# Gates in f32, shift sums as matmul rows, a softplus moved to the head, conditioning sums moved, and the chunk inverse applied inside the chain

## The chip, the cores and the metric

The kernel runs on one core of a Trainium2 chip. The metric is the device time of one execution in microseconds. Five engines work in parallel, each through its own queue: TensorE (PE, matmuls), VectorE (DVE, elementwise and scans), ScalarE (ACT, activations and copies), GpSimd (POOL) and SyncE (SP), which here issues nearly all DMAs.

## What is computed

Two residual layers of width 1024 over 1024 positions, and behind them a third, hybrid layer that the change does not touch. In front of the first two stands an RMS norm with a scale and a shift that come from a conditioning vector:

```
c_act = silu(c)
for i in range(2):
    cond = c_act @ ada_w[i] + ada_b[i]          # 1024 x 3072
    shift, scale, gate = cond[:D], cond[D:2*D], cond[2*D:]
    h = rmsnorm(x, norm_g[i]) * (1.0 + scale) + shift
    out = rglru_block(h) if i == 0 else gated_deltanet_block(h)
    x = x + gate * out
```

The first layer is a gated recurrence. Its gates are block-diagonal, eight blocks of 128x128:

```
xb, zg = split(h @ in_w);  xf = causal_conv4(xb) + conv_b
gates  = sigmoid(einsum('sni,knij->ksnj', xf, gate_w) + gate_b)      # r, i
log_a  = -8 * r * softplus(-lam);  a = exp(log_a)
b      = sqrt(-expm1(2 * log_a)) * (i * xf)
y      = scan(a, b) * silu(zg);   out = y @ out_w
```

The second is a gated delta rule with eight heads of 128, in chunks. Per chunk T is the inverse of a unit lower triangular matrix, and the state S passes from chunk to chunk:

```
w = T @ (k_beta * exp(g));  u = T @ v_beta
v_new = u - w @ S
o     = q_dec @ S + attn @ v_new
S     = S * e_last + k_dec.T @ v_new
```

## The kernel before

Activations lie transposed (channels on partitions). A projection is made of f16 products: the f32 weight is staged in `wst`, and `split` makes a high part `wh` (ACT) and a low part `wl` (DVE) of it; three matmuls of 512 columns (L111 to L113) add up to one f32 product. The framework fixes the order of the instructions on each engine ahead of time from the program's order, its priorities and buffers, and each engine runs its list in order.

*First layer.* A conditioning sum is made on DVE: a stage of `ada_w` (`sta`, 128x8x256, or `ast` and `wst_ada`) is multiplied by a column of `ccol` and accumulated, one instruction for each of eight row blocks (`ada_acc`, L148 and L150); transposes on PE (`ps_ada`) and a DVE reduction finish it into `adac`. `ada_load(0)` makes the shift so, and its f16 pair `shl` multiplies the projection weights once (`ps_sh`) for a bias. `xbranch(p)`, four of them, makes projection, convolution `xf` (L331), gates and scan for 256 channels; `zbranch(p)` makes the other half. Between them stand `ada_step()`s, which finish one pending sum (`ada_fin`, L185 to L189) and start the next. In `xbranch`, `xf` is split into `xh` and `xl`, and each gate is three matmuls (L501 to L503). The softplus of `lam` (`lamn`, some 33 small DVE instructions) is written ahead of the first `xbranch`. Two halves of one sum of the second layer (`ada_part(1, 2, h)`) stand in the loop of the output projection, `out0`.

*Second layer.* `dense(h)` makes q, k and v of a head, `stage1(h)` the products inside chunks, `base(h)` the inverse of the 32-blocks by 31 steps on DVE, `levels(h)` the larger blocks of the inverse `TdT` and behind them u (`ps_u`) and w (`ps_w`) of all eight chunks; `chain(h)` then goes over the chunks with the state S:

```
pe.matmul(ps1[:, :P], wT, S, start=True, stop=True)
pe.matmul(pso[:, :P], qT[:, c, :], S, start=True, stop=False)
dve.scalar_tensor_tensor(out=vn, in0=ps1[:, :P], scalar=nD[:, c:c + 1], in1=u, op0=ALU.mult, op1=ALU.add)
...
pe.matmul(psk[:, :P], kd, vn, start=True, stop=True)
```

The chain of head h is written ahead of `dense(h + 2)` and of the stages of head h + 1, and in the order its instructions lie between theirs.

Of the kernel before, what the change touches and what calls it, by code (L numbers as in the profile page):

```python
# [9 lines left out]
F16 = mybir.dt.float16  # L10
# [10 lines left out]
NK = 8  # L21
# [7 lines left out]
def kernel(ctx, tc, ins, out):  # L29
# [135 lines left out]
    def ada_sum(pl, tiles, l, part, h):  # L165
        acc = pl.tile([P, 512], F32, tag="ad", name="ad")
# [5 lines left out]
    def ada_part(pl, l, part, h):  # L172
        acc = pl.tile([P, 512], F32, tag="ad", name="ad", bufs=2)
# [173 lines left out]
    with ExitStack() as s0:  # L347
# [44 lines left out]

        G0 = pl.tile([P, NK], F32, name="G0")
# [6 lines left out]

        load_x(0)
        prows = load_cols(pl, PA, 0)
# [32 lines left out]
        ada_load(0)  # L435
# [7 lines left out]
    with ExitStack() as sy:  # L443
        ypool = mkpool("y0", stack=sy)
        yT = []
        with ExitStack() as s0:
# [4 lines left out]
            for g2 in range(2):  # L451
                gst = wstage("gst")
                sp.dma_start(gst[:, :D].rearrange("p (n j) -> p n j", n=NK),
                             a["lru_gate_w"][0, g2].rearrange("n i j -> i n j"))
                gh = pl.tile([P, D], F16, name=f"gwh{g2}")
                gl = pl.tile([P, D], F16, name=f"gwl{g2}")
                split(gh, gl, gst[:, :D], scale=WS)
                gw.append((gh, gl))
            lamn = pl.tile([P, NK], F32, name="lamn")
            sp.dma_start(lamn, a["lru_lambda"].rearrange("o (k p) -> p (o k)", p=P))  # L460
            dve.tensor_scalar(out=lamn, in0=lamn, scalar1=-1.0, scalar2=None, op0=ALU.mult)
            softplus(pl, lamn, spl, [P, NK], "sl")
            sp8 = cst.tile([P, NK], F32, name="sp8")
            sp4 = cst.tile([P, NK], F32, name="sp4")
            dve.tensor_scalar(out=sp8, in0=spl, scalar1=-8.0, scalar2=None, op0=ALU.mult)
            dve.tensor_scalar(out=sp4, in0=spl, scalar1=-4.0, scalar2=None, op0=ALU.mult)


            def xbranch(p, w):
                xf = xf0 if p == 0 else lru_xf(p, pl)  # L470
                xh = pl.tile(PR, F16, tag="xh", name="xh")
                xl = pl.tile(PR, F16, tag="xl", name="xl")
                if p > 0:
                    sb = shift_proj(w)
                for e in range(2 if p > 0 else 0):
# [4 lines left out]
                    split(xh[:, e], xl[:, e], xf[:, e])  # L480
                if p == 0:
                    sb = shift_proj(w)
                    for e in range(2):
# [7 lines left out]
                        split(xh[:, e], xl[:, e], xf[:, e])  # L491
                tg = []
                for g2 in range(2):
                    gx = pl.tile(PR, F32, tag=f"gt{g2}", name=f"gt{g2}")
                    gh, gl = gw[g2]
# [45 lines left out]
            adt, adp = [ada_fetch(pl, *adq.pop(0))], []  # L541

            def ada_step():
                if adp:
# [9 lines left out]
            ada_step()  # L554
            xbranch(1, wx[1])
            wx.append(load_w(a["lru_in_w"][0], 3 * WC))
            ada_step()
# [12 lines left out]
            zbranch(3, wz[3])  # L570
        with ExitStack() as s0:
# [7 lines left out]
            for i in range(NT + 1):  # L579
# [27 lines left out]
    with ExitStack() as s0:  # L607
# [28 lines left out]
        eg = gcol.tile([P, NT, NH], F32, name="eg")  # L636
# [7 lines left out]
        act.activation(eg, gc, AF.Exp)  # L644
# [27 lines left out]
        B3 = [P, 4, P]  # L672

        def bc(t, b):
            return t[:, 4 * b:4 * b + 4].unsqueeze(2).to_broadcast(B3)

        def dense(h):
# [3 lines left out]
            for nm in ("q", "k", "v"):  # L681
                xp = pl.tile([P, T + 3], F32, tag="xp", name="xp", bufs=2)
                xt = (pl if nm == "q" else plA).tile([P, T], F32, tag=nm + "T", name=nm + "T", bufs=3 if nm == "q" else 1)
# [14 lines left out]
        def stage1(h):  # L698
# [16 lines left out]
            nD = gcol.tile([P, NT], F32, tag="nD", name="nD", bufs=3)  # L715
# [3 lines left out]
            for n, src in ((0, kT), (1, qT)):  # L719
# [9 lines left out]
                if n == 0:  # L729
# [3 lines left out]
                    dve.tensor_scalar(out=nD, in0=Dc, scalar1=-1.0, scalar2=None, op0=ALU.mult)  # L733
# [41 lines left out]
            st_[h] = dict(qT=qT, attnT=E, U=U, kr=kr, vr=vr, Dc=Dc, nD=nD, rq=rq, Lp=Lp)  # L775
# [22 lines left out]
        def levels(h):  # L798
            d = st_[h]
            U, kr, vr, Dc = d["U"], d["kr"], d["vr"], d["Dc"]  # L800
# [47 lines left out]
            d["wT"], d["u"] = [], []  # L848
            for b in range(2):
                bs = slice(4 * b, 4 * b + 4)  # L850

                def lvl(lh, rh, nm):
                    ps = ps_c(nm)
                    for c in range(4):
                        pe.matmul(ps[:, P * c:P * (c + 1)], lh[:, c, :], rh[:, c, :], start=True, stop=True)
                    return ps.rearrange("p (c t) -> p c t", c=4)
# [3 lines left out]
                for c in range(4):  # L860
# [6 lines left out]
                d["wT"].append(wT)  # L867
                d["u"].append(u)

        def chain(h):  # L870
            d = st_.pop(h)
            qT, attnT, kr, nD, rq = d["qT"], d["attnT"], d["kr"], d["nD"], d["rq"]
# [5 lines left out]
            for c in range(NT):  # L878
                u, wT = d["u"][c // 4][:, c % 4, :], d["wT"][c // 4][:, c % 4, :]
                pso = ps_c("ps_o")  # L880
                if c == 0:
                    vn = u
                else:
                    ps1 = ps_c("ps_ws")
                    pe.matmul(ps1[:, :P], wT, S, start=True, stop=True)
                    pe.matmul(pso[:, :P], qT[:, c, :], S, start=True, stop=False)
                    vn = gcol.tile([P, P], F32, tag="vn", name="vn", bufs=2)
# [62 lines left out]
        def yload(q):  # L950
            if q < NH // 2 - 1:
                for e in range(2):
                    tag = ("kT", "vT", "GB", "Lp", "U", "vr")[2 * q + e]
                    yt = plA.tile([P, 2, T], F16, tag=tag, name="yo", bufs=2 if tag in ("U", "vr") else 1)
# [3 lines left out]
        dense(0)  # L958
        dense(1)
        for h in range(NH):  # L960
            stage1(h)
# [603 lines left out]
```

## Time and profile before

| | before |
|---|---|
| median of 3 runs | 1854.75 us (1852.91 to 1855.04) |
| profiled execution | 1849.51 us |
| its span | 1847.8 us |
| mean granted clock of TensorE | 0.985 of full speed |
| PE, DVE, ACT busy | 1740.0, 1451.2, 937.9 us |

The span runs from the first to the last instruction of the profiled execution; the 1.7 us around it are launch and end. Durations in the rows below are of that execution. Busy time counts an engine's instructions once where they overlap, so a matmul's duration is longer than the distance to the next one; where the text needs the price of a matmul in a full queue, it takes the distance of two starts. An f32 matmul leaves two records.

### The profile page before, as it was taken

Reading aid. Unit: us, or ns where it says so; the run is one execution under the profiler, and the core shown is the slowest. Engines: PE = TensorE matmul, PEld = TensorE weight load, DVE = VectorE, ACT = ScalarE, POOL = GpSimd, SP = SyncE. Lnnn points to the kernel's source line nnn. Section 1 sums busy time; section 2 is a strip of 40 time slices with the busy share of each in tenths; the row PEclk is TensorE's granted clock in tenths of the full one; section 3 lists DMA queues with packets and bytes.
Section 4 is the critical chain, followed back from the end, with each engine's and each line's share of the span. In section 5 each row is a group of like instructions: output and inputs, shape, how many; then the busy total and the mean of one; then the engine's idle time right before and its main releaser. Section 6 shows DMA issues by size and latency. Waiting matters only on the chain.

```text
span 1847.8 us, 29435 instructions
## 1 busy us (share of the span) xinstructions
PE 1740.0 (94%) x11719; PEld 1081.4 (59%) x11719; DVE 1451.2 (79%) x2480; ACT 937.9 (51%) x1669; POOL 66.2 (4%) x152
## 2 busy tenths in 40 slices
PE   4778999989899999999999999999999999999998
PEld 2333449845466655688889586555444444444487
DVE  5898778754898888988566799999999999593332
ACT  6477773345566766676453434655561221572221
POOL 0000010000000000001000110000000000000000
PEclk9889999999999999999999999999999999999999
DMA  9465336413131221335252411101321121111222
GB/s 312 161 156 129 69 103 199 138 55 83 32 92 45 56 77 44 95 110 152 81 183 81 99 49 49 53 19 53 125 80 35 48 90 50 42 33 59 80 70 92
DMA packets 157858, 165.25 MB, mean 89 GB/s; under 512 B 41886, under 2 KB 136158, under 8 KB 157722
## 3 DMA queue, kind: packets, MB, share of 16 engines
q1 hardware_dynamic: 156314, 159.17, 28.7%
q0 software_dynamic: 1408, 4.21, 0.6%
q8 instruction: 92, 1.51, 0.4%
q14 instruction: 44, 0.36, 0.1%
HBM read 139.05 MB, written 23.12 MB: 88 GB/s over the span
## 4 chain that ended last, share of the span: by engine, by line
PE 52%; DVE 30%; ACT 9%; issue 6%; DMA 2%; SPq 0%; POOL 0%; DVEq 0%; ACTq 0%; POOLq 0%
DVE cc L1035 5%; PE psmm L112 4%; PE psmm L111 4%; PE psmm L113 4%; DVE wl L105 3%; PE ps_out L120 2%; PE ps_out L118 2%; PE ps_out L119 2%; DVE tm L790 2%; DVE Tt L792 2%; PE ps_fin L120 2%; PE ps_fin L118 2%; PE ps_fin L119 2%; PE ps_zc L113 1%; PE ps_zc L111 1%
## 5 line engine op out<-in xcount | busy, mean ns | idle before, releaser
L111 PE MATMUL psmm<-hTh,wh 128*128 128x512 f16 x896 | 341.4, 382 | 7.8 <-ACT zs L533 5.3
L112 PE MATMUL psmm<-hTl,wh 128*128 128x512 f16 x896 | 342.0, 382 | 0.6 <-DVE hTl L398 0.6
L113 PE MATMUL psmm<-hTh,wl 128*128 128x512 f16 x896 | 341.7, 381 | 0.0
L1035 DVE SCALAR_TENSOR_TENSOR cc<-cu,cols,cc 128x1024 f32<-128x1024 f32 (+1 forms) x270 | 302.0, 1167 | 0.9
L112 PEld LDWEIGHTS <-wh 128*128 128x128 f16 x1568 | 154.0, 98 | 178.6 <-issue 10.9
L113 PEld LDWEIGHTS <-wl 128*128 128x128 f16 x1568 | 154.0, 98 | 176.0 <-issue 7.5
L111 PEld LDWEIGHTS <-wh 128*128 128x128 f16 x1568 | 154.0, 98 | 173.4 <-issue 6.9
L105 DVE SCALAR_TENSOR_TENSOR wl<-wst,wh 128x2048 f16<-128x2048 f32 (+2 forms) x71 | 153.9, 2171 | 69.8 <-ACT wh L104 69.8
L104 ACT ACTIVATE wh<-wst 128x2048 f16<-128x2048 f32 (+2 forms) x71 | 128.7, 1814 | 102.3 <-PE ps_gs L112 27.7
L790 DVE TENSOR_TENSOR tm<-Lp,Tt 128x248 f32<-128x248 f32 (+30 forms) x248 | 77.3, 312 | 4.1
L792 DVE TENSOR_TENSOR Tt<-Tt,tm 128x248 f32<-128x248 f32 (+30 forms) x248 | 76.7, 309 | 4.7
L119 PE MATMUL ps_z<-wh,hTl 128*128 128x256 f16 x256 | 69.8, 273 | 0.0
L118 PE MATMUL ps_z<-wh,hTh 128*128 128x256 f16 x256 | 69.8, 273 | 0.0
L120 PE MATMUL ps_z<-wl,hTh 128*128 128x256 f16 x256 | 69.8, 273 | 0.0
L118 PE MATMUL ps_fin<-wh,merged 128*128 128x256 f16 x256 | 69.8, 273 | 0.0
L119 PE MATMUL ps_fin<-wh,merged 128*128 128x256 f16 x256 | 69.8, 273 | 0.0
L120 PE MATMUL ps_fin<-wl,merged 128*128 128x256 f16 x256 | 69.8, 273 | 0.0
L119 PE MATMUL ps_out<-wh,hs 128*128 128x256 f16 x256 | 69.7, 273 | 0.0
L118 PE MATMUL ps_out<-wh,hs 128*128 128x256 f16 x256 | 69.7, 273 | 0.0
L120 PE MATMUL ps_out<-wl,hs 128*128 128x256 f16 x256 | 69.7, 273 | 0.0
L123 ACT ACTIVATE hTh<-ps_ht 128x512 f16<-128x512 f32 x32 | 17.4, 594 | 76.0 <-PE ps_ht L271 76.0
L727 ACT ACTIVATE jk<-ps_tk 128x128 f32<-128x128 f32 x128 | 35.7, 279 | 38.6 <-PE ps_tk L723 35.7
(539 smaller groups left out, 4085.9 us busy)
## 6 DMA issues: line engine op xcount, KB each, us to landing
wst<-in_w_in_dram SPq DMA_DIRECT2D x24, 1024.0 KB
wst<-in_gdn_in_w_dram SPq DMA_DIRECT2D x16, 1024.0 KB
ast<-in_ada_w_dram SPq DMA_DIRECT2D x24, 512.0 KB
xt<-in_x_dram SPq DMA_DIRECT2D x16, 512.0 KB
wst<-in_lru_in_w_dram SPq DMA_DIRECT2D x8, 1024.0 KB
sta<-in_ada_w_dram SPq DMA_DIRECT2D x8, 1024.0 KB
wst<-in_lru_out_w_dram SPq DMA_DIRECT2D x4, 1024.0 KB
wst_ada<-in_ada_w_dram SPq DMA_DIRECT2D x4, 1024.0 KB
```

The lines of the kernel that those rows point to most:

```text
L104: act.activation(hi, st, AF.Copy, scale=WS)
L105: dve.scalar_tensor_tensor(out=lo, in0=st, scalar=WS, in1=hi, op0=ALU.mult, op1=ALU.subtract)
L111: pe.matmul(ps, wh[:, k, c0:c0 + P], ah(k), start=(k == 0), stop=False)
L112: pe.matmul(ps, wh[:, k, c0:c0 + P], al(k), start=False, stop=False)
L113: pe.matmul(ps, wl[:, k, c0:c0 + P], ah(k), start=False, stop=(k == nk - 1))
L118: pe.matmul(ps, ah(k), wh[:, k, :], start=(k == 0), stop=False)
L119: pe.matmul(ps, al(k), wh[:, k, :], start=False, stop=False)
L120: pe.matmul(ps, ah(k), wl[:, k, :], start=False, stop=(k == nk - 1))
L727: act.activation(jk, pst[:, P * c:P * (c + 1)], AF.Square, accum_out=kq[:, n, 4 * b + c:4 * b + c + 1])
L790: dve.tensor_tensor(out=tv, in0=Lp[:, j, j + 1:].unsqueeze(1).to_broadcast([P, 8, n]), in1=Tt[:, :, j:j + 1].to_broadcast([P, 8, n]), op=A ...
L792: dve.tensor_tensor(out=Tt[:, :, j + 1:], in0=Tt[:, :, j + 1:], in1=tv, op=ALU.subtract)
L1035: dve.scalar_tensor_tensor(out=acc, in0=cus[j][:, i + t0:i + t0 + n], scalar=col("cw", j, i), in1=acc, op0=ALU.mult, op1=ALU.add)
```

## The change

1. Gates: the gate weights are loaded straight into f32 tiles `gw0` and `gw1` (no stage, no split), `xf` is no longer split, and each gate is one f32 matmul.
2. Shift sums: `ada_load(0)` becomes `ada_rows(0)`. A column of `ccol` is the stationary operand and a 256-column piece of `sta` the moving one, 32 matmuls in all; ACT copies the row of 1024 sums out in two halves (`adrow`), eight transposes of one column each (`ps_adc`) and a DVE addition bring it into `adac`.
3. Softplus: the load of `lamn` becomes the second on SP's queue, and the softplus is written ahead of the first norm.
4. Conditioning sums: the first fetch for the other parts stands behind `xbranch(1)` where it stood ahead of `xbranch(0)`, and two sums may be pending.
5. The part `ada_part(1, 2, h)` moves from `out0` to behind `dense(0)` of the second layer, and its end to ahead of `stage1(1)`.
6. Inverse: `levels` ends with `TdT`. `chain` computes `r = vr - exp(g) * (kT S)`, then `T r` by a matmul, and ACT scales it to `vn`. `kT`, `vr` and `TdT` live through the chain; `kT` has three buffers where it had one.

```diff
+        def ada_rows(part):
+            o = adac[:, part, :]
+            row = pl.tile([1, D], F32, name="adrow")
+            pss_ = [ps_s("ps_adr") for _ in range(2)]
+            for kk in range(4):
...
+                for k in range(NK):
+                    pe.matmul(r, ccol[:, k:k + 1], st[:, k, :], start=(k == 0), stop=(k == NK - 1))
+            for n in range(2):
+                act.activation(row[:, 512 * n:512 * (n + 1)], pss_[n][0:1, :], AF.Copy)
+            pst = ps_s("ps_adc")
+            for k in range(NK):
+                pe.transpose(pst[:, k:k + 1], row[0:1, P * k:P * (k + 1)], ident[0:1, 0:1])
+            dve.tensor_tensor(out=o, in0=pst[:, 0:NK], in1=cols[:, :, prow["ab"] + part], op=ALU.add)
...
+        lamn = pl.tile([P, NK], F32, name="lamn")
+        sp.dma_start(lamn, a["lru_lambda"].rearrange("o (k p) -> p (o k)", p=P))
         load_x(0)
+        dve.tensor_scalar(out=lamn, in0=lamn, scalar1=-1.0, scalar2=None, op0=ALU.mult)
+        softplus(pl, lamn, spl, [P, NK], "sl")
...
-        ada_load(0)
+        ada_rows(0)
...
-                gst = wstage("gst")
-                sp.dma_start(gst[:, :D].rearrange("p (n j) -> p n j", n=NK),
-                             a["lru_gate_w"][0, g2].rearrange("n i j -> i n j"))
...
-                split(gh, gl, gst[:, :D], scale=WS)
+                g_ = pl.tile([P, D], F32, name=f"gw{g2}")
+                sp.dma_start(g_.rearrange("p (n j) -> p n j", n=NK), a["lru_gate_w"][0, g2].rearrange("n i j -> i n j"))
...
-                    split(xh[:, e], xl[:, e], xf[:, e])
...
-                            pe.matmul(ps, gh[:, js], xh[:, e, HF[hf]], start=True, stop=False)
-                            pe.matmul(ps, gh[:, js], xl[:, e, HF[hf]], start=False, stop=False)
-                            pe.matmul(ps, gl[:, js], xh[:, e, HF[hf]], start=False, stop=True)
-                            act.activation(gx[:, e, HF[hf]], ps, AF.Sigmoid, scale=IWS, bias=col("lgb", j, g2))
+                            pe.matmul(ps, gw[g2][:, js], xf[:, e, HF[hf]], start=True, stop=True)
+                            act.activation(gx[:, e, HF[hf]], ps, AF.Sigmoid, bias=col("lgb", j, g2))
...
-            adt, adp = [ada_fetch(pl, *adq.pop(0))], []
+            adt, adp = [], []
             def ada_step():
-                if adp:
+                if len(adp) == 2 or not adt:
                     ada_fin(pl, *adp.pop(0))
...
-            ada_step()
             xbranch(1, wx[1])
+            adt.append(ada_fetch(pl, *adq.pop(0)))
...
-                if i in (5, 6):
-                    adp.append(ada_part(pl, 1, 2, len(adp)))
-            for q in adp:
-                ada_fin(pl, *q)
...
-                p3 = lvl(TdT[:, bs], vr[:, bs], "ps_u")
-                u = pl.tile(B3, F32, tag="u", name="u", bufs=3)
-                for c in range(4):
-                    act.activation(u[:, c, :], p3[:, c, :], AF.Copy, scale=Dc[:, 4 * b + c:4 * b + c + 1])
-                Tw = pl.tile(B3, F32, tag="X2", name="Tw")
-                dve.tensor_tensor(out=Tw, in0=TdT[:, bs], in1=bc(eg[:, :, h], b), op=ALU.mult)
-                p3 = lvl(kr[:, bs], Tw, "ps_w")
-                wT = pl.tile(B3, F32, tag="wT", name="wT", bufs=3)
-                act.activation(wT, p3, AF.Copy)
...
-                    pe.matmul(ps1[:, :P], wT, S, start=True, stop=True)
+                    pe.matmul(ps1[:, :P], kT[:, c, :], S, start=True, stop=True)
                     pe.matmul(pso[:, :P], qT[:, c, :], S, start=True, stop=False)
-                    dve.scalar_tensor_tensor(out=vn, in0=ps1[:, :P], scalar=nD[:, c:c + 1], in1=u,
+                    dve.scalar_tensor_tensor(out=r, in0=ps1[:, :P], scalar=neg[:, c, h:h + 1], in1=vr[:, c, :],
                                              op0=ALU.mult, op1=ALU.add)
+                pe.matmul(ps1[:, P:2 * P], TdT[:, c, :], r, start=True, stop=True)
+                vn = gcol.tile([P, P], F32, tag="vn", name="vn", bufs=2)
+                act.activation(vn, ps1[:, P:2 * P], AF.Copy, scale=Dc[:, c:c + 1])
...
         dense(0)
+        adp = [ada_part(pl, 1, 2, hf, "zs") for hf in range(2)]
         dense(1)
         for h in range(NH):
+            if h == 1:
+                for q in adp:
+                    ada_fin(pl, *q)
             stage1(h)
```

Two places in the order of PE's instructions. The first is in the first layer, before: the first of the sums' transposes (`ps_ada`) behind projections (`psmm`), with the next shift rows (`ps_sh`) behind it.

```order
L111 MATMUL psmm<-hTh,wh 128x512
...
L112 MATMUL psmm<-hTl,wh 128x512
...
L113 MATMUL psmm<-hTh,wl 128x512
L185 MATMUL ps_ada<-ident,ad 128x128 x4
...
L340 MATMUL ps_sh<-shl,wh 128x2
```

In the order of the changed kernel PE has, early in the same stage, the new rows (`ps_adr`) and the transposes of their sums (`ps_adc`) between projections:

```order
L113 LDWEIGHTS wl
L113 MATMUL psmm<-hTh,wl 128x512
L404 MATMUL ps_adr<-sta,ccol 1x256 x32
L409 MATMUL ps_adc<-ident,adrow 128x1 x4
L111 LDWEIGHTS wh
L111 MATMUL psmm<-hTh,wh 128x512
```

The 32 rows stand in one piece ahead of projections that stood ahead of the shift rows before, and the transposes of L185, which stood between the gates of the first block and those of the second, come behind the gates of the third.

The second place is one step of the chunk chain on PE in a middle head, before: `ps_ws` is the product with S, `ps_kv` the update of S, `ps_o` the output, and `psmm` projections of a later head.

```order
L885 MATMUL ps_ws<-S,wT 128x128
L886 MATMUL ps_o<-S,qT 128x128
...
L111 MATMUL psmm<-hTh,wh 128x512
...
L112 MATMUL psmm<-hTl,wh 128x512
L894 MATMUL ps_kv<-vn,kd 128x128
L902 MATMUL ps_o<-vn,E 128x128
...
L113 MATMUL psmm<-hTh,wl 128x512
```

The same step in the changed kernel, where `ps_r` takes both the product with S and the one with the inverse:

```order
L863 MATMUL ps_r<-S,kT 128x128
L864 MATMUL ps_o<-S,qT 128x128
...
L112 MATMUL psmm<-hTl,wh 128x512
...
L113 MATMUL psmm<-hTh,wl 128x512
L868 MATMUL ps_r<-r,TdT_3467 128x128
...
L111 MATMUL psmm<-hTh,wh 128x512
...
L112 MATMUL psmm<-hTl,wh 128x512
...
L113 MATMUL psmm<-hTh,wl 128x512
L875 MATMUL ps_kv<-vn,kd 128x128
L883 MATMUL ps_o<-vn,E 128x128
```

Where a step had two groups of projections between its own matmuls, it now has three.

## Rows read from the trace of the kernel before

**Rows 1.** the first part of the page: busy us, share, instructions

```profile
PE 1740.0 (94%) x11719; PEld 1081.4 (59%) x11719; DVE 1451.2 (79%) x2480; ACT 937.9 (51%) x1669; POOL 66.2 (4%) x152
```

**Rows 2.** view by windows: length, then busy time of each engine, granted clock

```profile
66.00:100.00 34.00, 23.48 (x157) 11.10 (x158) 33.59 (x96) 15.80 (x21) 0.20 (x2) 0.85 0.61 196
100.00:150.00 50.00, 36.49 (x245) 17.87 (x244) 46.46 (x47) 39.62 (x42) 2.31 (x5) 0.86 0.66 141
150.00:200.00 50.00, 45.33 (x202) 19.92 (x201) 37.34 (x32) 38.77 (x43) 0.47 (x2) 0.97 0.32 95
465.00:935.00 470.00, 450.26 (x3770) 315.54 (x3769) 384.64 (x1026) 305.48 (x821) 25.20 (x46) 1.00 0.29 81
```

**Rows 3.** view of waits, PE, 60 to 180 us: total, times, longest

```profile
PE ps_ada L185 <- DVE shr L344: 10.6, 1, 10.6
...
PE ps_gate L501 <- ACT xh L123: 4.7, 1, 4.7
PE ps_sh L340 <- DVE shl L438: 3.5, 1, 3.5
```

**Rows 4.** timeline, 130 to 135 us: start, duration, engine, line

```profile
130.56 0.74 DVE L150 SCALAR_TENSOR_TENSOR ad<-ast,ccol,ad 128x512 f32<-128x512 f32 x1
...
131.45 1.09 PE L185 MATMUL ps_ada<-ident,ad 128*128 128x128 f32 x4 [10.55 <-DVE shr L344]
...
134.54 0.63 PE L502 MATMUL ps_gate<-xl,gwh 128*128 128x512 f16 x1
...
134.97 0.63 PE L503 MATMUL ps_gate<-xh,gwl 128*128 128x512 f16 x1
```

**Rows 5.** timeline of PE near 1589 us: one f32 matmul among f16 ones

```profile
1588.63 1.02 PE L1455 MATMUL ps_mean<-lnsm,ones 128*128 128x512 f32 x2
1589.48 0.38 PE L111 MATMUL ps_gc<-hTh,wh 128*128 128x512 f16 x1
1589.70 0.38 PE L112 MATMUL ps_gc<-hTl,wh 128*128 128x512 f16 x1
```

**Rows 6.** groups by line: count, busy, mean ns, idle; 40-100 us, then all

```profile
L150 DVE SCALAR_TENSOR_TENSOR accs<-sta,ccol,accs 128x256 f32<-128x256 f32 x28 | 11.9, 488 | 0.0
...
L125 DVE TENSOR_TENSOR xl<-xf,xh 128x1024 f16<-128x1024 f32 x8 | 9.8, 1222 | 5.9 <-ACT xh L123 5.9
```

**Rows 7.** timeline of the head, and a group of the softplus

```profile
0.81 0.46 SPq L143 DMA_DIRECT2D ccol<-in_c_dram  x1
...
10.78 0.17 DVE L256 TENSOR_SCALAR ss<-ss 128x4 f32<-128x4 f32 x1 [10.78 <-ACT jk L360]
...
L91 DVE SCALAR_TENSOR_TENSOR slq<-slq,sle 128x8 f32<-128x8 f32 x7 | 1.2, 167 | 0.2
```

**Rows 8.** groups by line, whole program: products behind the levels

```profile
L855 PE MATMUL ps_w<-Tw,kr 128*128 128x128 f32 x128 | 17.6, 280 | 0.7 <-DVE Tw L863 0.7
...
L855 PE MATMUL ps_u<-vr,TdT 128*128 128x128 f32 x128 | 17.4, 279 | 0.6 <-DVE TdT L847 0.6
...
L863 DVE TENSOR_TENSOR Tw<-TdT,eg 128x512 f32<-128x512 f32 x16 | 10.9, 683 | 1.2 <-PE ps_w L855 0.8
```

**Rows 9.** timeline, 638 to 641 us: one step of a head's chunk chain

```profile
638.13 0.38 PE L885 MATMUL ps_ws<-S,wT 128*128 128x128 f32 x2
...
638.35 0.39 PE L886 MATMUL ps_o<-S,qT 128*128 128x128 f32 x2
...
638.62 0.35 DVE L888 SCALAR_TENSOR_TENSOR vn<-ps_ws,nD,u 128x128 f32<-128x128 f32 x1
...
639.11 0.46 PE L894 MATMUL ps_kv<-vn,kd 128*128 128x128 f32 x2
...
640.98 1.91 ACT L104 ACTIVATE wh<-wst 128x2048 f16<-128x2048 f32 x1 [0.36 <-PE psmm L112]
```

**Rows 10.** moved sums as a group; chain that ended last from 465 us

```profile
L150 DVE SCALAR_TENSOR_TENSOR ad<-wst_ada,ccol,ad 128x512 f32<-128x512 f32 x14 | 10.4, 746 | 0.1
...
467.78 8.75 DMA GB<-gb_d
```

More of the change, by code (lines that the diff above doesn't have):

```diff
@@ L170, in ada_sum, with ada_part @@
         return acc, l, part, h
-    def ada_part(pl, l, part, h):
-        acc = pl.tile([P, 512], F32, tag="ad", name="ad", bufs=2)
+    def ada_part(pl, l, part, h, tag):
+        acc = pl.tile([P, 512], F32, tag=tag, name="ad", bufs=2)
         for kk in range(2):
@@ L391, in ada_load @@
                     then(kk, ks)
+        def ada_rows(part):
[3 more added lines that the diff above has]
+            for kk in range(4):
+                st = pl.tile([P, 2 * D], F32, tag="sta", name="sta", bufs=4).rearrange("p (k c) -> p k c", k=NK)
+                c0 = D * part + 2 * P * kk
+                sp.dma_start(st, a["ada_w"][0, :, c0:c0 + 2 * P].rearrange("(k p) c -> p k c", p=P))
+                r = pss_[kk // 2][0:1, 256 * (kk % 2):256 * (kk % 2 + 1)]
+                for k in range(NK):
[6 more added lines that the diff above has]
+            dve.tensor_tensor(out=o, in0=pst[:, 0:NK], in1=cols[:, :, prow["ab"] + part], op=ALU.add)
         G0 = pl.tile([P, NK], F32, name="G0")
@@ L399, in put_hT @@
                                      op0=ALU.mult, op1=ALU.subtract)
+        lamn = pl.tile([P, NK], F32, name="lamn")
+        sp.dma_start(lamn, a["lru_lambda"].rearrange("o (k p) -> p (o k)", p=P))
         load_x(0)
+        dve.tensor_scalar(out=lamn, in0=lamn, scalar1=-1.0, scalar2=None, op0=ALU.mult)
+        softplus(pl, lamn, spl, [P, NK], "sl")
+        sp8 = cst.tile([P, NK], F32, name="sp8")
+        sp4 = cst.tile([P, NK], F32, name="sp4")
+        dve.tensor_scalar(out=sp8, in0=spl, scalar1=-8.0, scalar2=None, op0=ALU.mult)
+        dve.tensor_scalar(out=sp4, in0=spl, scalar1=-4.0, scalar2=None, op0=ALU.mult)
         prows = load_cols(pl, PA, 0)
@@ L451 @@
             for g2 in range(2):
-                gst = wstage("gst")
-                sp.dma_start(gst[:, :D].rearrange("p (n j) -> p n j", n=NK),
-                             a["lru_gate_w"][0, g2].rearrange("n i j -> i n j"))
-                gh = pl.tile([P, D], F16, name=f"gwh{g2}")
-                gl = pl.tile([P, D], F16, name=f"gwl{g2}")
-                split(gh, gl, gst[:, :D], scale=WS)
[L458 to L466, printed above, removed]
+                g_ = pl.tile([P, D], F32, name=f"gw{g2}")
+                sp.dma_start(g_.rearrange("p (n j) -> p n j", n=NK), a["lru_gate_w"][0, g2].rearrange("n i j -> i n j"))
+                gw.append(g_)
             def xbranch(p, w):
                 xf = xf0 if p == 0 else lru_xf(p, pl)
-                xh = pl.tile(PR, F16, tag="xh", name="xh")
-                xl = pl.tile(PR, F16, tag="xl", name="xl")
                 if p > 0:
@@ L570 @@
             zbranch(3, wz[3])
+            ada_step()
+            while adp:
+                ada_step()
         with ExitStack() as s0:
@@ L643 @@
         act.activation(el.rearrange("p i h -> p (i h)"), psg[:, 64:128], AF.Exp)
-        act.activation(eg, gc, AF.Exp)
+        neg = gcol.tile([P, NT, NH], F32, name="neg")
+        act.activation(neg, gc, AF.Exp)
+        dve.tensor_scalar(out=neg, in0=neg, scalar1=-1.0, scalar2=None, op0=ALU.mult)
         act.activation(kd1, kd1, AF.Exp)
@@ L847, in levels @@
             dve.tensor_scalar(out=TdT[lo, :, hi], in0=px[lo], scalar1=-1.0, scalar2=None, op0=ALU.mult)
[L848 to L853, printed above, removed]
-                    for c in range(4):
-                        pe.matmul(ps[:, P * c:P * (c + 1)], lh[:, c, :], rh[:, c, :], start=True, stop=True)
-                    return ps.rearrange("p (c t) -> p c t", c=4)
-                p3 = lvl(TdT[:, bs], vr[:, bs], "ps_u")
-                u = pl.tile(B3, F32, tag="u", name="u", bufs=3)
-                for c in range(4):
-                    act.activation(u[:, c, :], p3[:, c, :], AF.Copy, scale=Dc[:, 4 * b + c:4 * b + c + 1])
-                Tw = pl.tile(B3, F32, tag="X2", name="Tw")
-                dve.tensor_tensor(out=Tw, in0=TdT[:, bs], in1=bc(eg[:, :, h], b), op=ALU.mult)
-                p3 = lvl(kr[:, bs], Tw, "ps_w")
-                wT = pl.tile(B3, F32, tag="wT", name="wT", bufs=3)
-                act.activation(wT, p3, AF.Copy)
-                d["wT"].append(wT)
-                d["u"].append(u)
         def chain(h):
             d = st_.pop(h)
-            qT, attnT, kr, nD, rq = d["qT"], d["attnT"], d["kr"], d["nD"], d["rq"]
+            qT, kT, attnT, kr, vr, Dc, rq = (d[n] for n in ("qT", "kT", "attnT", "kr", "vr", "Dc", "rq"))
+            TdT = TdTs[h % 2]
             o = pl.tile([P, NT, P], F32, tag="o", name="o", bufs=2)
```

26 lines of the change are left out of this document (8 added, 18 removed).

## The prediction

> **What bounds the kernel now.** I read the busy times first: TensorE (PE) is busy 94% of the span, VectorE (DVE) 79%, ScalarE (ACT) 51% [rows 1]. PE is the first suspect, but a share of the whole span says nothing of the stages that change, so the next view is the one by windows [rows 2]. From 66 to 200 us, the first layer's x and z branches, PE is busy 23.48 of 34, 36.49 of 50 and 45.33 of 50 us: 10.52 + 13.51 + 4.67 = 28.7 us idle, at a granted clock of 0.85 to 0.86 in the first two, so partly at 1.2 GHz and partly at 2.4. DVE is full there (33.59 of 34, 46.46 of 50). In the eight heads of the gated delta layer, 465 to 935 us, PE is busy 450.26 of 470 at clock 1.00. A change can win in the first stage by removing waits of PE, in the second mostly by removing PE work.
>
> The list of PE's waits names the idle time [rows 3]: 10.6 us before L185, the transposes that finish a conditioning sum, 4.7 before the gates' first matmul (for `xh`), and 3.5 before the shift rows' matmuls (for `shl`). The first is the longest and needs a second look: its releaser is given as the tiny `shr`, but the timeline has the last `ad` accumulation on DVE at 130.56 + 0.74 = 131.30 and the transposes at 131.45 [rows 4]. PE takes its instructions in order, so everything behind those four transposes waited for a DVE sum that nobody needed yet.
>
> **The change, part by part**, against the profiled execution's 1849.51 us (span 1847.8), which is 5.2 below the median of the runs. I make the sum as a difference and add it to the median.
>
> *Head (softplus first).* One more small load stands in SP's queue before the x rows; the same kind of load of 8 columns, `ccol`, takes 0.46 us to issue [rows 7], and so all loads behind it go out 0.46 us later. The softplus is 33 DVE instructions of about 0.167 us, 5.5 us; DVE does nothing before 10.78 us [rows 7], so it fits if `lamn` lands by 5. If it lands 2 us later, 2 us show. Between 0 and +2.5, I take **+0.7**, since the issue delay is certain and the rest is not. The Trainium skill ("DMA: Bandwidth & Descriptors", the table at its head) asks for pieces of 512 bytes for full rate, and this load is made of 4-byte pieces; no row here shows what such pieces do to the x rows behind them, and the sum by it would stay within the same bounds.
>
> *Shift sums on PE.* 28 accumulations of 128x256 on DVE go (11.9 us [rows 6]), with four first terms and the reductions. PE gets 32 f32 matmuls of one stationary column and 256 moving columns. No such form is in the trace. The nearest is an f32 matmul over 512 columns, L1455: 1589.48 - 1588.63 = 0.85 us, where f16 over 512 takes 0.22 [rows 5]. Half the columns give 0.43 each. From below, f16 at half the columns is 0.11 each, 3.5 us in all; from above, all 32 at 1.2 GHz, 0.85 each, 27.4 us. I take 0.43, the row of the same type: **13.7 us of PE work**. The order puts them 34 projection matmuls behind the columns' set-up, ahead of the two pieces of the projection, so most of them lie where PE still had work, and the work they push back fills what was idle.
>
> *Gates in f32.* Three f16 matmuls of 0.22 become one of 0.85: 0.20 more, x32 = **6.5 us of PE work**. Off DVE go eight `xl` splits (9.8 us [rows 6]) and the two weight splits, and ACT loses the same number of conversions. The chain `xf`, `xh`, `xl`, matmul becomes `xf`, matmul, so the 4.7 us wait for `xh` has no object any more. What is late next is `xf` itself, whose conv runs on the same DVE that does less before it. The gate weights now land straight in f32 tiles; they are issued after three weight stages, and if they are later than `xf`, they take its place.
>
> *Conditioning sums later.* Nothing is computed less. But the first finish of a sum (L185) moves from between the first and the second block's gates to behind the third block's, and a second sum may be pending before one is finished. The 10.6 us wait in front of it goes; PE's next work there is projections whose inputs are on hand.
>
> *First layer together.* The three waits are 10.6 + 4.7 + 3.5 = 18.8 us. PE gains 13.7 + 6.5 = 20.2 us of work. Those two cancel, +1.4. Of the other 28.7 - 18.8 = 9.9 us idle I let half close, -5.0, because DVE, which was full, loses some 22 us between 45 and 150 (11.9 of sums, 5.5 of softplus, half of the `xl`). And the clock: gate matmuls behind a wait stood 134.97 - 134.54 = 0.43 apart [rows 4] instead of 0.22; some 15 of them, 15 x 0.21 = 3 us, are at full clock if PE has not stood still before. **-6.5** (from +15, nothing but the three waits closing and the rows twice as dear, to -12, all idle time gone: 20.2 - 28.7 - 3.2).
>
> *One conditioning part into the next layer.* 14 accumulations of 0.746 us (10.4 us [rows 10]) and two first terms leave DVE in the output projection, where PE is the full engine: **-1** (0 to -2). They come into DVE's queue between the first heads' projections, with four loads of 1 MB behind the heads' weights. The stage has a wait of 8.75 us for `GB` in the chain [rows 10] in which they can hide if the queue's order lets them, and otherwise they delay the second head by up to 11 us: **+2**, most of it hidden.
>
> *Inverse in the chunk chain.* Out of each head go 16 f32 matmuls, `ps_u` and `ps_w` (256 records, two for a matmul, in eight heads [rows 8]), and two DVE products `Tw` (0.683 each). In come 8 matmuls T·r per head. An f32 matmul of 128 columns takes 638.35 - 638.13 = 0.22 us [rows 9], so PE loses 8 x 8 x 0.22 = **14.3 us** net in a stretch where it is 96% busy. ACT trades `u` for `vn`, one for one. The price is a third hop in a serial chain: now it goes matmul, DVE `vn`, matmul, DVE `S`; afterwards matmul, DVE `r`, matmul, ACT `vn`, matmul, DVE `S`. One hop of now takes from the matmul at 638.13 to the next at 639.11, 0.98 us [rows 9], and 2 x 0.22 of the chain's own matmuls and 2 x 0.215 of the next heads' projections fill 0.87 of it: 0.11 stands still. The order of after has two or three projections in each of the three hops, so I give each new hop the same 0.11: 64 x 0.11 = 7.0. **-7.3** for the eight heads (-14.3 if nothing stands still).
>
> *Sum*: 0.7 - 6.5 - 1 + 2 - 7.3 = -12.1; 1854.75 - 12.1 = **1843 us** (1837 for a run like the profiled one).
>
> **The rivals.**
> 1. *Everything is covered.* PE fills all 28.7 idle us, and the new hops stand still nowhere: -11.7 - 14.3 + 1.7 = -24.3, **1830**. For it: PE has projections waiting in both stages. Against: DVE stays the first layer's fuller engine after the scans start.
> 2. *The third hop is the bound (slower).* An uncovered hop costs 0.98 - 0.22 = 0.76, 64 of them 49 us. With all other terms at -4.8, the change loses from (14.3 + 4.8) / 64 = 0.30 us of standstill per new hop on, little more than one projection matmul missing; half of the hops bare give -4.8 - 14.3 + 24.3 = +5, **1860**, all of them 1884. For it: ACT's queue now holds a link of the chain, and in it stand weight conversions of 1.91 us [rows 9], in the order of after between one `vn` and the next too. Against: DVE has such conversions (`wl`) between links already. The Trainium skill ("TensorE: Matmul & The Clock Gate", the part on the array's architecture) says that ACT and DVE are strictly in order; by it no `vn` passes such a conversion; no row here shows ACT taking one out of order.
> 3. *The rows are slow.* The 32 row matmuls follow a wait for their loads and run at 1.2 GHz, 27.4 us instead of 13.7: the first layer gives +7.2 and the sum +1.6, **1856**.
> 4. *No real change.* PE bounds both stages, the first layer only trades idle time for work (0 instead of -6.5) and the hops stand still 0.2 us each, 12.8 instead of 7.0: +0.2, **1855**. For it: 20.2 us of new PE work against 18.8 of waits.
>
> **How the numbers follow.** Chances: forecast 0.40, rival 1 0.16, rival 2 0.17, rival 3 0.10, rival 4 0.17. A run of this kernel is told from no change at about 0.2%, 3.7 us. Faster: forecast, rival 1, and what of 3 and 4 comes out a little better, 0.61. Same: most of rival 4 and some of 3, 0.18. Slower: rival 2 and the rest, 0.21. The range 1825 to 1862 takes in rival 1 and the half-bare chain; left out are the fully bare chain and a preamble at its upper bound on top. The forecast's own range is 1836 to 1849.
>
> **What the profile would show.** Right: no PE wait before the conditioning transposes and the gates in 66 to 200 us; the first gate matmul several us earlier; 32 row matmuls within about 14 us; PE busy some 436 us in the heads' stretch, which is 5 to 12 us shorter; a chunk's step of nearly 3 us where it was 2. Wrong: rows at 0.85 us each at half the clock; PE waits for `vn` of more than 0.3 us per step; the wait for `GB` grown by the moved sums; ACT busy with `wh` while a T·r result lies in PSUM.

## The result and the profile after

The changed kernel takes 1865.21 us (median of 5 runs, 1861.03 to 1867.88) against 1854.97 before: ratio 1.0057, 95% interval 1.0041 to 1.0072. It is slower by 10 us where 1843 was forecast, and outside the range. The trace of the kernel before is of a run 5 us below its median, so a few us between two traces need not be the change.

The page's line of busy times, as [rows 1]:

```profile
PE 1755.8 (94%) x11623; PEld 1078.4 (58%) x11623; DVE 1411.8 (76%) x2408; ACT 921.0 (49%) x1643; POOL 64.8 (3%) x152
```

The windows, as [rows 2], with the stages behind them (the heads of the second layer now start some 15 us later):

```profile
66.00:100.00 34.00, 33.92 (x202) 15.28 (x201) 22.25 (x34) 22.18 (x27) 0.10 (x1) 1.00 0.72 232
100.00:150.00 50.00, 47.61 (x281) 22.28 (x279) 38.13 (x29) 38.79 (x39) 0.20 (x2) 0.97 0.23 76
150.00:200.00 50.00, 49.53 (x244) 22.93 (x243) 32.59 (x27) 37.50 (x40) 0.10 (x1) 1.00 0.13 43
...
275.00:300.00 25.00, 14.36 (x116) 12.46 (x117) 11.06 (x11) 0.00 (x0) 5.51 (x5) 0.80 0.48 82
275.00:385.00 110.00, 92.07 (x791) 80.85 (x792) 68.78 (x103) 25.28 (x43) 10.58 (x14) 0.91 0.47 138
480.00:945.00 465.00, 440.32 (x3649) 300.83 (x3647) 360.32 (x992) 292.04 (x793) 26.24 (x45) 0.98 0.29 79
```

From 66 to 200 us PE's idle time fell from 28.7 to 0.08 + 2.39 + 0.47 = 2.9 us, at a clock of 0.97 to 1.00: what was forecast for the first layer happened, and more of it. The last scan of the layer comes 11.4 us earlier. In the kernel before:

```profile
265.49 2.26 DVE L522 TENSOR_TENSOR_SCAN hs<-gt,at 128x1024 f32<-128x1024 f32 x1
```

In the changed kernel:

```profile
254.13 2.27 DVE L529 TENSOR_TENSOR_SCAN hs<-gt,at 128x1024 f32<-128x1024 f32 x1
```

The first matmul of the output projection (`ps_out`) comes 7.2 us earlier, at 268.6 where it was 275.8. The loss lies behind it. From 275 to 300 us PE is busy 14.36 of 25 us at a clock of 0.80, and from 275 to 385 us, which takes in the output projection and some 20 us behind it, 92.07 of 110, where the kernel before has:

```profile
275.00:385.00 110.00, 104.45 (x1063) 91.06 (x1062) 78.88 (x123) 32.51 (x50) 8.04 (x15) 0.97 0.46 150
```

The list of PE's waits from 60 to 300 us has one long entry, where [rows 3] had three:

```profile
PE ps_ada L185 <- DVE ad L150: 11.6, 1, 11.6
```

It is the same kind of wait as the one that [rows 4] showed at 131 us, 10.6 long: PE stands in front of the transposes that finish a conditioning sum. There it was the second of six sums; now it is the last, the wait is 11.6 long, and it stands at the end of the layer, with the matmuls of the output projection behind it in PE's queue. The timeline around it (start, duration, engine, line):

```profile
272.68 0.75 POOL L189 DMA_DIRECT2D ada_d<-adac  x1 [1.62 <-DVE adac L187]
...
274.20 2.42 DVE L150 SCALAR_TENSOR_TENSOR ad<-ast,ccol,ad 128x512 f32<-128x512 f32 x3 [1.81 <-DMA ast<-in_ada_w_dram]
...
283.76 0.33 SPq L277 DMA_DIRECT2D hn<-ada_d  x1
...
283.95 1.54 DVE L150 SCALAR_TENSOR_TENSOR ad<-ast,ccol,ad 128x512 f32<-128x512 f32 x2 [6.55 <-DMA ast<-in_ada_w_dram]
...
285.64 1.08 PE L185 MATMUL ps_ada<-ident,ad 128*128 128x128 f32 x4 [11.62 <-DVE ad L150]
...
287.95 0.77 POOL L189 DMA_DIRECT2D ada_d<-adac  x1 [11.86 <-DVE adac L187]
...
296.53 0.33 SPq L277 DMA_DIRECT2D SH<-ada_d  x1
...
296.91 0.42 SPq L289 DMA_DIRECT2D xt<-in_x_dram  x1
```

Read it downward. The last sum's loads were issued late (the four on SP's queue between 259.9 and 266.8 us), since their stages came free only as the sum ahead used them up; DVE waits 1.81 and 6.55 us for them. PE transposes at 285.64, GpSimd (POOL) stores the result to `ada_d` at 287.95, and the load of the shift row `SH`, which reads it back, starts on SP's queue at 296.53. Behind `SH` on that queue stands the load of the residual x, `xt`, which waits for nothing itself. The chain that ended last has the same steps, with their lengths:

```profile
287.95 8.51 DMA ada_d<-adac
...
296.91 6.21 DMA xt<-in_x_dram
303.22 0.69 DVE xt L296
```

The first residual sum, L296, is at 303.22. The kernel before had it, and the last of these six stores, at

```profile
255.63 0.75 POOL L189 DMA_DIRECT2D ada_d<-adac  x1 [23.38 <-DVE adac L187]
...
286.09 0.69 DVE L296 SCALAR_TENSOR_TENSOR xt<-rtmp,xt 128x512 f32<-128x512 f32 x1
```

So the residual sum is 17 us later, from a layer that ended 7 to 11 us earlier, and the last store left 20 us ahead of the projection before and leaves 19 us behind its start now. The sizes of the two new kinds of work were as forecast: the 32 rows, where an f32 matmul leaves two records,

```profile
62.04 13.97 PE L404 MATMUL ps_adr<-sta,ccol 128*1 128x256 f32 x64
75.94 0.40 PE L409 MATMUL ps_adc<-ident,adrow 1*128 1x1 f32 x4
```

take 75.94 - 62.04 = 13.9 us (13.7 forecast).

### The profile page after: what moved, and what is told of

Same layout as the page of the kernel before. It is cut to its first block, busy times and chain, and to the rows that moved or that the text cites. A ratio compares the mean times of both kernels' runs of the same rounds, so it can differ in the third digit from the quotient of the medians.

```text
span 1863.5 us, 29045 instructions
## 1 busy us (share of the span) xinstructions
PE 1755.8 (94%) x11623; PEld 1078.4 (58%) x11623; DVE 1411.8 (76%) x2408; ACT 921.0 (49%) x1643; POOL 64.8 (3%) x152
## 4 chain that ended last, share of the span: by engine, by line
PE 53%; DVE 27%; ACT 9%; issue 5%; DMA 4%; POOL 0%; SPq 0%; DVEq 0%; ACTq 0%; POOLq 0%
DVE cc L1021 5%; PE psmm L112 3%; PE psmm L111 3%; PE psmm L113 3%; DVE wl L105 2%; PE ps_out L118 2%; PE ps_out L119 2%; PE ps_out L120 2%; PE ps_fin L119 2%; PE ps_fin L118 1%; PE ps_fin L120 1%; PE ps_zc L113 1%; PE ps_zc L111 1%; PE ps_zc L112 1%; DVE tm L789 1%
## 5 line engine op out<-in xcount | busy, mean ns | idle before, releaser
L789 DVE TENSOR_TENSOR tm<-Lp,Tt 128x248 f32<-128x248 f32 (+30 forms) x248 | 73.3, 295 | 3.9
L791 DVE TENSOR_TENSOR Tt<-Tt,tm 128x248 f32<-128x248 f32 (+30 forms) x248 | 72.5, 292 | 4.7
L118 PE MATMUL ps_out<-wh,yo 128*128 128x256 f16 x192 | 53.0, 276 | 1.5 <-ACT wh L104 1.5
```

Of the source, the lines that this page charges most:

```text
L118: pe.matmul(ps, ah(k), wh[:, k, :], start=(k == 0), stop=False)
L789: dve.tensor_tensor(out=tv, in0=Lp[:, j, j + 1:].unsqueeze(1).to_broadcast([P, 8, n]), in1=Tt[:, :, j:j + 1].to_broadcast([P, 8, n]), op=A ...
L791: dve.tensor_tensor(out=Tt[:, :, j + 1:], in0=Tt[:, :, j + 1:], in1=tv, op=ALU.subtract)
```

## The experiments

Three theories stood at the start. **A**: the conditioning sums of part 4 end too late, and their way through memory and SP's queue holds up the output projection. **B**: the third hop of the chunk chain makes the heads slower (the forecast's own rival). **C**: the sums of part 5 hold up the first heads. Each experiment has its own runs of the kernel before beside it; ratios are to those, with a 95% interval. The ratios compare means, and differences in us are worked out from them (times some 1853 us), so they can differ a little from the difference of two medians.

**1. Part 4 undone.** In the changed kernel:

```diff
-            adt, adp = [], []
+            adt, adp = [ada_fetch(pl, *adq.pop(0))], []
...
-                if len(adp) == 2 or not adt:
+                if adp:
...
+            ada_step()
             xbranch(1, wx[1])
-            adt.append(ada_fetch(pl, *adq.pop(0)))
             wx.append(load_w(a["lru_in_w"][0], 3 * WC))
+            ada_step()
...
-            ada_step()
-            while adp:
-                ada_step()
```

> The changed kernel with part 4 alone undone: the conditioning sums are fetched ahead of the first block again and one is pending at a time. Theory A (the late sums: the last two are finished behind the last z branch, written out by GpSimd at 272.7 and 288.0 us and landed at 296.5, and the x rows of the residual stand behind them on SP's queue): the 24 us that the output projection loses between 276 and 303 us are gone, but the wait of PE for the first sum (10.6 us in the kernel before) may come back; 1843 to 1853 us. Theory B (the chunk chain's third hop) and theory C (the part moved into the next layer): nothing changes by more than 4 us, 1861 to 1869.

1840.56 us, ratio 0.9935 (0.992 to 0.995): 1.2% or 23 us below the changed kernel. It is below even theory A's range of 1843 to 1853, and B and C predicted no change, so theory A holds. PE's waits from 60 to 300 us, and the output projection's window:

```profile
PE ps_gate L510 <- DVE xf L331: 6.5, 3, 2.8
PE ps_ada L185 <- DVE ad L150: 1.3, 2, 1.0
```

```profile
275.00:385.00 110.00, 109.57 (x1061) 90.69 (x1059) 82.17 (x136) 32.11 (x53) 11.31 (x15) 0.98 0.47 155
```

PE is busy 109.57 of 110 us there. And the wait for a sum, 10.6 us in [rows 3], does not come back: 1.3 us. Parts 1 to 3 close it without part 4, as experiment 5 shows too; that they do it by taking work off DVE fits (DVE is busy 99.28 us from 66 to 200 there, where [rows 2] add up to 117.39), but was not tried by itself.

**2. The x loads first.** In the changed kernel the first three loads of the residual are issued ahead of those that read the sums back:

```diff
+            xpre = [out_x(pl, x_in[TS[i], :]) for i in range(3)]
             GA = bcast_row(pl, ada_d[0, 2 * D:3 * D], "GA")
             G, SH = load_mod(pl, 1)
```

> The changed kernel with the loads of the first three residual x tiles issued ahead of the loads of gate, scale and shift on SP's queue, nothing else. Theory A, and its detail that the queue on SP is what holds the residual: the first residual sum comes at about 293 instead of 303 us, and the norm then waits for the shift row (297 and the time it takes to land); 1855 to 1861 us. If the residual waited for something else, or under B and C: 1862 to 1868, no change.

1853.72 us, ratio 1.0002 (0.9988 to 1.0015), some 10 us below the changed kernel, lower than either expectation. SP's queue and DVE:

```profile
270.71 3.34 SPq L289 DMA_DIRECT2D xt<-in_x_dram  x1
...
293.57 0.68 DVE L300 TENSOR_TENSOR rtmp<-ps_out,GA 128x512 f32<-128x512 f32 x1
...
294.28 0.69 DVE L301 SCALAR_TENSOR_TENSOR xt<-rtmp,xt 128x512 f32<-128x512 f32 x1
...
298.10 0.33 SPq L277 DMA_DIRECT2D SH<-ada_d  x1
```

The first residual sum, now L301, is at 294.28 where the changed kernel has 303.22, and `xt` no longer waits; `SH` is as late as in the changed kernel (298.10), since the sum itself is, and PE still waits 9.2 us in front of the last sum's transposes (at 286.99). So of the 23 us about 10 belong to the queue on SP, and the rest, which goes with early sums (experiments 1 and 6), to the sum's lateness.

**3. The chain alone.** The kernel before with part 6 only.

> The kernel before with part 6 alone, the inverse inside the chunk chain. My step (8 matmuls fewer per head, 0.11 us of standstill per new hop): 1847.5, between 1841 and 1852. Theory B (the new hop is bare): 1860 or more. From the trace of the changed kernel, whose heads 3 to 7 gain 3.4 us each and whose first and last two lose: 1843 to 1855.

1853.49 us, ratio 1.0007 (0.9996 to 1.0019): no change, between my -7 and theory B, and just above the first range; only the range read from the changed kernel's trace holds. One step of the chain in the last head, where nothing but the output gate's projections (`ps_z`) stands between:

```profile
917.57 0.49 PE L859 MATMUL ps_r<-S,kT 128*128 128x128 f32 x2
...
918.10 0.35 DVE L862 SCALAR_TENSOR_TENSOR r<-ps_r,neg,vr 128x128 f32<-128x128 f32 x1 [0.58 <-PE ps_r L859]
...
918.51 0.38 PE L864 MATMUL ps_r<-r,TdT 128*128 128x128 f32 x1
...
919.03 0.37 ACT L866 ACTIVATE vn<-ps_r,Dc 128x128 f32<-128x128 f32 x1 [0.86 <-PE ps_r L864]
...
919.45 0.38 PE L871 MATMUL ps_kv<-vn,kd 128*128 128x128 f32 x1
...
919.98 0.35 DVE L876 SCALAR_TENSOR_TENSOR S<-S,el,ps_kv 128x128 f32<-128x128 f32 x1 [1.53 <-PE ps_kv L871]
...
920.38 0.38 PE L859 MATMUL ps_r<-S,kT 128*128 128x128 f32 x1
```

Three hops: 0.94 (to T·r), 0.94 (to `ps_kv`) and 0.93 us, 2.81 a step. The same head before has 1.99 from one step to the next:

```profile
921.70 0.49 PE L885 MATMUL ps_ws<-S,wT 128*128 128x128 f32 x2
...
923.69 0.49 PE L885 MATMUL ps_ws<-S,wT 128*128 128x128 f32 x2
```

So the new hop takes as long as an old one. That alone is not its cost, for PE can do projections meanwhile. In a middle head the link on ACT can stand behind a weight conversion:

```profile
637.80 1.91 ACT L104 ACTIVATE wh<-wst 128x2048 f16<-128x2048 f32 x1 [0.31 <-PE psmm L112]
...
637.83 0.38 PE L864 MATMUL ps_r<-r,TdT 128*128 128x128 f32 x1
...
639.62 0.35 ACT L866 ACTIVATE vn<-ps_r,Dc 128x128 f32<-128x128 f32 x1
...
640.10 0.40 PE L871 MATMUL ps_kv<-vn,kd 128*128 128x128 f32 x2
```

T·r is issued at 637.83, and `vn` runs at 639.62, behind the `wh` of 1.91 us; that step takes 5.4 us, from 636.94 to 642.35. That ACT takes its queue strictly in order is what the Trainium skill states ("TensorE: Matmul & The Clock Gate", the part on the array's architecture), and this row agrees. But PE does not stand still in this step: nine projection matmuls lie between T·r and `ps_kv`, and eight between the output's matmuls and the next step. The list of PE's waits from 468 to 942 us, which names those longer than 0.15 us, has one for `vn`, and none for `r`:

```profile
PE ps_kv L871 <- ACT vn L866: 1.7, 1, 1.7
```

Over the eight heads PE is busy

```profile
468.00:942.00 474.00, 448.66 (x3664) 304.91 (x3663) 370.15 (x1001) 296.05 (x802) 24.54 (x43) 0.98 0.29 81
```

that is 448.66 of 474 us, where [rows 2] has 450.26 of 470: 14.3 us of matmuls are gone, but PE is busy only 1.6 us less and idle 5.6 us more. Idle time and the clock (0.98 for 1.00) have taken their place.

**4. The part moved back.** The changed kernel with part 5 undone (the two `ada_part` again in the loop of `out0`).

> The changed kernel with part 5 alone undone: the two halves of the next layer's gate stand in the output projection again. Theory C (their 16 accumulations and the transposes that wait for them cost the first two heads 8 to 13 us): 1853 to 1858. Theory A: the output projection stays late, and with these sums back in it DVE has 11.5 us more there; 1862 to 1872.

1861.93 us, ratio 1.0052 (1.0037 to 1.0067), against 1.0057 of the changed kernel: no difference that can be told. Theory C falls, which asked for 7 to 12 us less than the changed kernel; theory A's range was missed by a tenth of a us.

**5. Parts 1 to 3 alone.** The kernel before with gates, rows and softplus changed, the rest as it was.

> The kernel before with parts 1 to 3 alone (gates in f32, shift sums as rows, softplus first). The changed kernel with early sums came out 12.6 us below the kernel before; the chain alone gave nothing and the moved part cost about 3. So, if the parts add up, these three give 13 to 16 us: 1837 to 1841. If the moved sums of part 5 were what makes room in the output projection, or the parts only work together: 1845 to 1850.

1846.99 us, ratio 0.9968 (0.9956 to 0.9979), -5.9 us: less than the parts' sum required, and in the second range, for parts that do not add up. PE's waits and two windows:

```profile
PE ps_gate L510 <- DVE xf L331: 7.1, 3, 2.8
...
PE ps_ada L185 <- DVE ad L150: 1.2, 2, 1.0
```

```profile
66.00:200.00 134.00, 128.06 (x708) 59.67 (x707) 99.28 (x106) 97.35 (x103) 2.89 (x7) 0.97 0.49 134
275.00:385.00 110.00, 105.28 (x1054) 90.44 (x1052) 80.82 (x126) 34.56 (x52) 7.77 (x14) 0.95 0.51 169
```

Here too the wait for the sums is 1.2 us without part 4. PE is busy 128.06 of 134 us in the first layer's branches (105.3 before), and 105.28 of 110 in the second window, about as before (104.45).

**6. Early, with two pending.** The changed kernel with part 4's second half alone: the first fetch ahead of the first block as before, two sums pending.

> The changed kernel with the conditioning sums fetched as early as before, but two pending before one is finished, and a finish only at the step after. Theory A: the place of the last store decides, and it lies two branches earlier than in the changed kernel and one later than with one pending; the loss in the output projection is gone or at most 5 us: 1840 to 1847. If a second pending sum is itself the cost (SBUF, SP's queue): above 1855.

1846.72 us, ratio 0.9963 (0.9948 to 0.9978): some 17 us below the changed kernel, but above experiment 1; the last of the six stores goes out at 270.0 us, where experiment 1 has 262.0 and the changed kernel 287.9. So of part 4's 23 us some 17 come from the later fetch and some 5 from the second pending sum.

**7. Freed work without the new hop.** The kernel before, `wT` copied from the keys in place of the product w:

```diff
-                Tw = pl.tile(B3, F32, tag="X2", name="Tw")
-                dve.tensor_tensor(out=Tw, in0=TdT[:, bs], in1=bc(eg[:, :, h], b), op=ALU.mult)
-                p3 = lvl(kr[:, bs], Tw, "ps_w")
...
-                act.activation(wT, p3, AF.Copy)
+                act.activation(wT, kr[:, bs], AF.Copy)
```

> The kernel before with the product w left out (its 8 matmuls, the scaling of the inverse on VectorE), wT being a copy of the transposed keys instead, so the output is not the reference's; the chain keeps its two hops. It frees as much of TensorE and VectorE as part 6 does. If TensorE's work is what sets the heads' time and the third hop ate the gain: 1838 to 1842 (14 us of matmuls, 11 of VectorE). If the heads' time is set by the serial stages and not by the work: 1849 to 1853.

1848.75 us, ratio 0.997 (0.9953 to 0.9987), -5.6 us (-2.4 to -8.7), a miss of both expectations: 14.3 us less of PE and 10.9 less of DVE are worth about 6 together (the medians differ by 3.8). So the freed work gives back some 0.4 of PE's part, between 0.2 and 0.6. Part 6 frees as much and came to +0.7 per thousand, so its hop costs about what the freed work gives: 0.37% between the two, 6.9 us (3 to 11), or 0.11 us for each of 64 hops.

**8. The link on DVE.** Experiment 3 with `vn` on VectorE:

```diff
-                act.activation(vn, ps1[:, P:2 * P], AF.Copy, scale=Dc[:, c:c + 1])
+                dve.tensor_scalar(out=vn, in0=ps1[:, P:2 * P], scalar1=Dc[:, c:c + 1], scalar2=None, op0=ALU.mult)
```

> The kernel before with part 6 alone, and in it the scaling of T r to vn on VectorE instead of ScalarE. If the weight conversions in ScalarE's queue (1.9 us) are what stretches the steps of the chain beyond 2.8 us: 1845 to 1850. If the floor of three hops is what costs, or VectorE's own queue holds the link up as often: 1852 to 1858.

1873.53 us, ratio 1.0108 (1.0091 to 1.0124), worse than both expectations. The group of the link, from 470 to 960 us:

```profile
L866 DVE TENSOR_SCALAR vn<-ps_r,Dc 128x128 f32<-128x128 f32 x64 | 22.3, 349 | 10.9 <-PE ps_r L864 10.4
```

Its 64 instructions add 22.3 us of work and 10.9 us of waiting to an engine that works through the next head's inverse in the same queue. That fits the 20 us, but how they come about was not followed further; the conversions on ACT are the smaller evil.

**9 and 10. Which of parts 5 and 6.** Parts 1, 2, 3 and 5, and parts 1, 2, 3 and 6, both with early sums.

> Parts 1, 2, 3 and 5, the sums as early as before, the chain as before. Parts 1 to 3 alone stand at -5.6 us against the kernel before, parts 1, 2, 3, 5 and 6 with early sums at -12.6, part 6 alone at 0. If the 7 us between them are part 5's (sums taken out of the output projection, which was 6 us shorter in the trace with early sums): 1839 to 1843. If part 6 is worth something only when its fillers change: 1846 to 1850.

> Parts 1, 2, 3 and 6, the sums as early as before, the gate's two halves in the output projection as before. If part 5 is what gives the 7 us: 1845 to 1850, as parts 1 to 3 alone. If part 6: 1839 to 1843.

1839.06 us, ratio 0.9921 (0.9894 to 0.9947), and 1841.27, ratio 0.9942 (0.9923 to 0.9962). Both are lower than parts 1 to 3 alone, the second only just beyond the noise, and experiment 1 with both parts (0.9935) is no lower than either. So neither reading holds: each of the two parts gives something beside parts 1 to 3, and the second gives nothing on top of the first. What part 5 does to PE shows in two windows, the output projection and the 25 us from 360, most of them behind it. Without it (experiment 5), then with it (experiment 9):

```profile
275.00:360.00 85.00, 84.64 (x775) 76.09 (x773) 67.20 (x107) 27.20 (x41) 3.77 (x7) 1.00 0.56 187
360.00:385.00 25.00, 20.64 (x281) 14.35 (x280) 13.62 (x21) 7.37 (x11) 3.99 (x7) 0.80 0.36 107
```

```profile
275.00:360.00 85.00, 85.00 (x780) 76.74 (x779) 60.73 (x92) 23.89 (x40) 3.77 (x7) 1.00 0.42 140
360.00:385.00 25.00, 24.64 (x290) 14.10 (x288) 22.10 (x47) 7.52 (x14) 2.56 (x6) 1.00 0.59 198
```

The projection was full with the sums in it; PE gains 0.4 us there and 4.0 behind it. Experiment 1 beside experiment 10, the same pair with part 6 in both, has the same rows (24.64 of 25 against 19.80) and no gain in time that can be told, so these rows do not say what the part is worth. For part 6 beside parts 1 to 3 no such row was found.

**11. The finish later.** Experiment 1 with the moved sums finished ahead of the fourth head instead of the second, for its trace has, from 400 to 520 us,

```profile
PE ps_tk L721 <- DVE adac L186: 8.0, 1, 8.0
```

> Parts 1, 2, 3, 5 and 6 with early sums, and the finish of the moved sums ahead of the fourth head instead of the second. The trace has 8.0 us in which TensorE waits for it ahead of the second head's transposes. If that wait is on the path: 1832 to 1836. If the stage has another wait right behind it (the base of the second head on VectorE): 1838 to 1841.

1840.34 us, ratio 0.9932 (0.991 to 0.9954), against 0.9935. That wait is 0.3 us in its trace, and the time is the same: the 8.0 us of waiting were not on the path.

**12. All remedies.** The changed kernel with an early fetch and two pending, the x loads first, the finish later.

> The changed kernel with the sums fetched early and two pending, the x loads ahead of gate, scale and shift on SP's queue, and the finish of the moved sums ahead of the fourth head. With two pending the first layer ended 7.7 us ahead of the kernel before and lost all of it ahead of the first residual sum. If the SP queue is what held it: 1833 to 1839. If the shift row itself comes too late: 1840 to 1846.

1838.52 us, ratio 0.9919 (0.9887 to 0.9951), in the range for the queue on SP: 8 us below experiment 6, which has no x loads first and the finish earlier. It and experiment 9 have the lowest times, but are not told apart from each other or from experiments 1, 10 and 11; all of these lie below both kernels.

## Why the prediction was wrong, step by step

*Conditioning sums later.* This step failed. It read "Nothing is computed less [...] The 10.6 us wait in front of it goes", took that wait as a gain, and gave the part no cost. It did not ask who waits for the end of the sums. The six sums are the gate that the output projection needs, and the scale and shift of the norm behind it; they go out through `ada_d` and come back, and SP's queue holds the x loads behind them. The wait did not go either: it moved to the last sum, 11.6 us long, in front of the output projection. The part costs 23 us (experiment 1), some 10 of them by SP's queue (experiment 2), and gains nothing, for the wait at 131 us goes without it (experiments 1 and 5). The trace of the kernel before had what was needed: the last store comes only 20 us ahead of the projection, so there was little room to move it.

*Head.* +0.7 forecast; PE's first projection starts 1.1 us later in the changed kernel's trace, and 0.6 to 1.1 later in the others that have the part. Right.

*Rows and gates.* 13.7 and 6.5 us of PE work forecast; the rows measured 13.9, and 60 of 64 records of the gates stand 0.43 to 0.53 apart, 0.86 a matmul. Right. Parts 1 to 3 give -5.9 where head and first layer were put at -5.8. The size is right, but part 4 was counted in it, for the 10.6 us wait: that this wait closes without part 4 was luck.

*The moved part.* +1 forecast as the sum of -1 and +2. Measured, it depends on what else is there: about -8.7 us beside parts 1 to 3 (0.9921 against 0.9968, give or take 5), -1.3 where part 6 is there too (experiments 1 and 10, within the noise), nothing in the changed kernel (experiment 4). The -1 for the output projection fits the rows, for PE was full there already (84.64 of 85 us). The stretch behind the projection, where PE gains 4 us, had no term, and the +2 of delay in the heads is not seen: the 8.0 us that PE waits for the moved sums were not on the path (experiment 11). Why the parts do not add up stays open.

*The chain.* -7.3 forecast; alone it measured +0.7 per thousand, +1.3 us (-0.7 to +3.5). The term that was mis-sized is the freed work: 14.3 us forecast (64 x 0.22 is rather 14.1), 5.6 measured (experiment 7), though PE is busy 96% of that stretch. Why the rest does not come back stays open; in the rows, idle time at other waits and a lower clock stand in its place. The price of the hop, 7.0 us forecast, comes to 6.9 by the difference of experiments 3 and 7, so nothing shows that term to be wrong. A step grew from 1.99 to 2.81 us, and to 5.4 where a conversion stands in ACT's queue, but "nearly 3 us where it was 2" was forecast too, and projections fill these steps. Rival 2 named the right place, ACT's queue; its bare hops did not come, since PE waited for `vn` once, 1.7 us long, in experiment 3, and in the changed kernel's list of waits not at all.

*The sum.* It was -12.1, with no cost for part 4, and experiment 1, which leaves that part out, measures -0.65%, -12.0 us. That agreement is in part luck: parts 1 to 3 are as forecast, and parts 5 and 6 together give -6 where +1 and -7.3 were forecast, but part 5 by itself gives -8.7 beside parts 1 to 3, and part 6 -4.8 (experiment 10).

## What to carry to other kernels

When a computation is moved later to clear a queue, find the first reader of its result and follow the whole way there, with each DMA and each load that stands in an issuing queue behind a waiting one; a load that needs nothing belongs ahead of one that waits. A wait of an in-order engine can be closed from either end: look whether another part of the change already makes the producer earlier. And before freed work of a busy engine is priced at its own length, take it away alone and see what the stage gives back. The length of a step in a chain is not its price either: what counts is how long the busy engine stands still in it.

## What was not expected of the hardware

A store of 2 KB from a tile of 128 x 4 to memory on GpSimd's queue took 8.3 to 13.4 us from issue to landing (eight of them, median 10.3) in the changed kernel, and 8.1 to 11.5 in the kernel before. So writing out half of a sum takes longer than the DVE work that makes it, some 5.7 us (one instruction of 0.48 and seven of 0.75). An f32 matmul with a stationary operand of one column took 0.43 us for 256 columns, half of what 512 columns take with 128 stationary columns (0.86): the width of the stationary operand saved nothing. While PE waited from 275 to 300 us its granted clock fell to a mean of 0.80.
